# A transformer block on one core: the last matrix product by row tiles, the residual added by transfers, the row factors asked for last

## The chip, the cores and the metric

The kernel runs on one core of a Trainium2 chip. That core has a matrix engine (PE, TensorE), a vector engine (DVE), a scalar engine (ACT), a general engine (POOL, GpSimd) and a queue engine (SP) that mostly issues DMA transfers; ACT and POOL can issue transfers too, on queues of their own. Each engine runs its instructions strictly in the order in which they were put into its program, so an instruction that waits holds everything behind it on that engine. The metric is the device time of one execution in microseconds (us).

## What is computed

The block is one layer of a flow-matching backbone on 512 tokens of width 2048: a modulated norm, a combined input projection for gated linear attention and a gated short convolution, an output projection with a gated residual, then a second modulated norm, a SwiGLU feed-forward with hidden width 5632 and another gated residual, and a final norm. The change lies in the last three of these, cut to what matters:

```python
x_next = x + gt1 * mix                                   # 512 x 2048
h2 = modulate(rmsnorm(x_next, norm2_g), sh2, sc2)
x_next = x_next + gt2 * ((silu(h2 @ wg) * (h2 @ wu)) @ wd)   # wd: 5632 x 2048
out = rmsnorm(x_next, final_g)    # x * rsqrt(mean(x*x, row) + 1e-6) * final_g
```

`gt2` and `final_g` are vectors over the 2048 columns; the norm's factor is one number for each of the 512 rows.

## The kernel before, in words

**Products in pieces.** Operands are float32 and are split into a high and a low part in a reduced format (`split`: ACT casts the high part, L102, DVE subtracts to get the low part, L103), and three matmuls replace one (`mm3`). The order within `mm3` is low part of the stationary operand by high part of the weights, high by low, high by high; the first matmul of a product thus needs only the cast of the weights, the second needs DVE's low part as well.

**Seven products for eight.** The product with `wd` runs in 2 by 2 blocks by `seven`, which needs seven block products with sums and differences of blocks. The hidden width is cut into three groups (`GROUPS`: `nu` = 4, 4 and 3 units of 2 x 256), and for each group `g` the output columns are cut into two halves `p` of 1024. For each `(g, p)`, `seven` goes through steps "1", "5", "63", "7", "24", or in the last one (`g` = 2, `p` = 1, called `fast`) "1", "5", "63", "2", "7", "4". In each step and for each unit `u` it asks for a weight tile (512 KB: `held` into `ch` in steps 1 and 5, `load_raw` into `raw` in steps 63 and 24, four buffers), forms differences of weight tiles on DVE, splits, and runs 12 matmuls of 512 columns. Stationary operands A11, S1, S2, S4, S3, A12, A22 (tiles `a0` to `a6`, a high and a low part each) were written to memory earlier (`opd`) and are brought back by `load_ops`, 256 KB each, by SP.

**What sets the order.** SP's program follows the order in which the kernel's code asks for loads. The `before` table of `seven` names places, a step or a step and a unit, at which something is asked for ahead of that step. On the other engines the tile framework's scheduler places the instructions by its own estimates of time; the written order is only its input.

**The end of a column block.** `upd` adds a finished accumulator to the output tiles `y[row tile][column block]` (128 x 512 each, 4 row tiles by 4 blocks). When the last addition to a tile is done, `finish_block` loads the block's saved residual `xnd` into a tile of pool `big` (SP, L1110), multiplies `y` by `gt2` (DVE, L1111), adds the residual (DVE, L1112), and squares and sums it (ACT, L1113). When the second half of the columns has the blocks of a pair of row tiles, `finish_rows` works out the row factors (`row_scale`: a reduction, a chain of 128 x 2 operations on DVE and a square root on ACT) and multiplies eight tiles by row factor and `final_g` at once (DVE, L1120), each followed by its output transfer from POOL (L1121).

## Time and profile before

| what | value |
| --- | --- |
| time, median of 3 runs | 2346.79 us (2343.20 to 2351.29) |
| the profiled execution | 2344.56 us, its span 2342.8 us |
| granted TensorE clock, mean | 0.986 |
| PE busy | 2257.2 us, 96% of the span |
| DVE / ACT / POOL busy | 1667.6 / 1012.4 / 139.3 us |
| DMA | 431.43 MB, mean 184 GB/s |

The span runs from the first to the last instruction in the trace. A row of a timeline has the start, the duration, the engine, the line, the operation with output and inputs, how many instructions stand in the row, and in brackets how long the engine was idle ahead of it and which instruction ended that. `SPq` is SP's queue of transfers to issue. A row of a table of windows has the busy time and count of each engine in a stretch of the span, then the clock granted to PE (PEclk), the busy share of the 16 DMA engines and what they moved.

### The profile page before, as it was taken

The page shows a single profiled execution, that of the slowest core. Times are in us where ns is not written, and L with a number is a line of the kernel's source. Part 1 is how long each engine was busy: PE and PEld are TensorE (multiplying, and loading weights), DVE is VectorE, ACT ScalarE, POOL GpSimd, SP SyncE. Part 2 cuts the span into 40 slices and gives each one's busy share as a digit, 9 for nine tenths or more (in the row PEclk, how much of TensorE's full clock was granted, in tenths as well). Part 3 has the DMA queues.
Part 4 walks back from the last instruction along what each step waited for, and adds up shares of the span by engine and source line. Part 5 has one row for each costly group of instructions (what it writes and reads, how often), then busy time and mean ns, then how long its engine had stood idle before and what let it go on. Part 6 is the DMA issues. An engine that isn't in the chain of part 4 may idle for free.

```text
span 2342.8 us, 27643 instructions
## 1 busy us (share of the span) xinstructions
PE 2257.2 (96%) x10232; PEld 1794.3 (77%) x10232; DVE 1667.6 (71%) x2046; ACT 1012.4 (43%) x1365; POOL 139.3 (6%) x186
## 2 busy tenths in 40 slices
PE   8999999999989999989999999999999999999996
PEld 4766667787877778767888888888888878888875
DVE  3566164655655757769888788878887867787898
ACT  3432155233232334485554555455545544443343
POOL 2433000000000000000000000000000000000001
PEclk9999999999999999989999999999999999999998
DMA  9774465665656654533434643464346585755634
GB/s 329 229 245 135 144 225 162 206 194 190 221 187 204 191 179 172 188 107 128 160 123 147 207 144 123 147 206 144 122 148 207 187 316 173 279 181 192 253 128 143
DMA packets 161620, 431.43 MB, mean 184 GB/s; under 512 B 17868, under 2 KB 38636, under 8 KB 161357
## 3 DMA queue, kind: packets, MB, share of 16 engines
q1 hardware_dynamic: 141612, 380.87, 49.1%
q0 software_dynamic: 8720, 28.58, 3.2%
q10 hardware_dynamic: 11152, 20.21, 2.3%
q8 instruction: 81, 1.33, 0.2%
q14 instruction: 55, 0.44, 0.1%
HBM read 380.82 MB, written 48.78 MB: 183 GB/s over the span
## 4 chain that ended last, share of the span: by engine, by line
issue 42%; PE 10%; DVE 2%; POOL 2%; ACT 1%; DMA 0%; POOLq 0%; ACTq 0%; DVEq 0%
PE acc L90 10%; POOL opd L1002 1%; DVE wlo L103 1%; POOL out L1121 0%; PE pt L988 0%; DVE ch L812 0%; ACT big L906 0%; ACT whi L102 0%; DMA raw<-wu 0%; DVE a4l L103 0%; DVE s L739 0%; DVE a6l L103 0%; DVE ch L793 0%; DVE a3l L103 0%; DVE ch L798 0%
## 5 line engine op out<-in xcount | busy, mean ns | idle before, releaser
L102 ACT CAST whi<-ch 128x1024 fp32r<-128x1024 f32 x350 | 368.8, 1055 | 425.9 <-PE acc L90 348.5
L103 DVE TENSOR_TENSOR wlo<-ch,whi 128x1024 fp32r<-128x1024 f32 x350 | 426.1, 1222 | 139.0 <-ACT whi L102 137.9
L102 ACT CAST whi<-raw 128x1024 fp32r<-128x1024 f32 x252 | 264.1, 1052 | 414.9 <-PE acc L90 244.9
L103 DVE TENSOR_TENSOR wlo<-raw,whi 128x1024 fp32r<-128x1024 f32 x252 | 308.9, 1227 | 186.6 <-ACT whi L102 186.1
L374 DVE CUSTOM_DVE_ANT_0 raw<-raw,cbc 128x1024 f32<-128x1024 f32 x128 | 156.4, 1224 | 190.1 <-DMA raw<-wm 187.6
L90 PE MATMUL acc<-hhl,whi 128*128 128x512 f32 x640 | 201.6, 396 | 0.0
L90 PE MATMUL acc<-hhi,wlo 128*128 128x512 f32 x320 | 135.8, 426 | 14.0 <-DVE wlo L103 13.0
L90 PEld LDWEIGHTS acc<-hhl,whi 128*128 128x128 f32 x640 | 122.3, 191 | 28.2 <-issue 2.5
L90 PE MATMUL acc<-whi,a6l 128*128 128x512 f32 x312 | 122.5, 394 | 8.5 <-ACT whi L102 7.5
L90 PE MATMUL acc<-hhl,wlo 128*128 128x512 f32 x320 | 128.3, 401 | 0.0
L90 PE MATMUL acc<-hlo,whi 128*128 128x512 f32 x320 | 127.7, 399 | 0.2 <-DVE hlo L108 0.2
L90 PE MATMUL acc<-hhi,whi 128*128 128x512 f32 x320 | 127.4, 398 | 0.0
L90 PE MATMUL acc<-wlo,a6h 128*128 128x512 f32 x312 | 123.0, 394 | 2.2 <-DVE wlo L103 2.1
L90 PE MATMUL acc<-wlo,a0h 128*128 128x512 f32 x312 | 122.6, 393 | 2.1 <-DVE wlo L103 2.1
L90 PE MATMUL acc<-whi,a6h 128*128 128x512 f32 x312 | 122.3, 392 | 0.0
L90 PE MATMUL acc<-whi,a5l 128*128 128x512 f32 x312 | 121.9, 391 | 0.0
L90 PE MATMUL acc<-wlo,a5h 128*128 128x512 f32 x312 | 121.7, 390 | 0.0
L90 PE MATMUL acc<-whi,a5h 128*128 128x512 f32 x312 | 121.6, 390 | 0.0
L90 PE MATMUL acc<-whi,a0h 128*128 128x512 f32 x312 | 121.5, 389 | 0.0
L90 PE MATMUL acc<-whi,a0l 128*128 128x512 f32 x312 | 121.3, 389 | 0.0
L90 PE MATMUL acc<-whi,a2l 128*128 128x512 f32 x280 | 109.1, 392 | 4.8 <-ACT whi L102 4.8
L90 PE MATMUL acc<-wlo,a2h 128*128 128x512 f32 x280 | 110.2, 394 | 1.4 <-DVE wlo L103 1.4
(305 smaller groups left out, 4747.6 us busy)
## 6 DMA issues: line engine op xcount, KB each, us to landing
raw<-wm SPq DMA_DIRECT2D x128, 512.0 KB, 4.7
raw<-wu SPq DMA_DIRECT2D x92, 512.0 KB, 3.8
ch<-wu SPq DMA_DIRECT2D x88, 512.0 KB, 4.0
raw<-wc SPq DMA_DIRECT2D x48, 512.0 KB, 4.0
raw<-wd SPq DMA_DIRECT2D x47, 512.0 KB, 6.0
ch<-wd SPq DMA_DIRECT2D x44, 512.0 KB, 5.9
opd<-oh ACTq DMA_DIRECT2D x77, 256.0 KB, 3.0
opd<-ol POOLq DMA_DIRECT2D x77, 256.0 KB, 3.3
```

What stands on the lines that cost most here:

```text
L90: nc.tensor.matmul(o, l, r, start=start, stop=stop, skip_group_check=True)
L102: nc.scalar.copy(hi, src)
L103: (eng or nc.vector).tensor_tensor(lo, src, hi, op=ALU.subtract)
L374: nc.vector.tensor_tensor_reduce(out=w, in0=w, in1=cbc[:, hf * 1024 : hf * 1024 + 1024], scale=1.0, scalar=0.0, op0=ALU.mult, op1=ALU.add, ...
L1002: nc.gpsimd.dma_start(opd[j][i, 1].rearrange("p k t -> p (k t)"), lo.bitcast(F32))
```

## The change

There are four edits, all in the product with `wd`.

1. In the first half of each group's columns (`p` = 0), the loads of S3 (`a4`) are asked for in step "63" ahead of its last unit, and those of A12 and A22 (`a5`, `a6`) ahead of step "7". Before, S3 came ahead of step "5", and A12 and A22 ahead of step "63".
2. `finish_block` no longer loads the residual into a tile of its own and no longer adds it on DVE. `residual` multiplies `y` by `gt2` on DVE, and a transfer issued by POOL adds `xnd` into `y` (`accum_op`). The square on ACT and a new multiplication by `final_g` on DVE follow it.
3. `finish_rows` applies the row factors on ACT, eight plain scalings, instead of with `final_g` on DVE.
4. In the last projection the last step is "4r": the splits of its three weight tiles come first, then all products of row tile 0, then all of row tile 1, and after each of the two `finish_tile` does the rest of that row tile: scale, add, square, `final_g`, a row factor of its own, and four scalings shared by ACT and DVE, with the output transfers on SP, POOL and ACT. The residuals of these two tiles are put in earlier, ahead of step "7".

```diff
@@ seven
-        def product(i, u, r, acc, first):
+        def parts(r):
             hi = wpool.tile([P, 1024], F32R, tag="whi", name="whi", bufs=3)
             lo = wpool.tile([P, 1024], F32R, tag="wlo", name="wlo", bufs=3)
             split(hi, lo, r)
+            return hi, lo
+
+        def product(i, u, r, acc, first, rows=(0, 1)):
+            hi, lo = r if type(r) is tuple else parts(r)
             if first and u == 0:
                 acc += [bank8("acc"), bank8("acc")]
-            for t in range(2):
+            for t in rows:
...
                     if "4" in step:
                         tt(a[u], c, a[u], op=ALU.subtract)
+                    if step == "4r":
+
+                        b[u] = parts(a[u])
+                        for t in range(2) if end else ():
+                            for v in range(nu):
+                                product(A22, v, b[v], X, False, (t,))
+                            after["c21"](t, X[t])
+                    elif "4" in step:
                         product(A22, u, a[u], X, False)
@@ the product with wd
             def before_63():
...
-                if p == 0:
-                    load_ops(g, A12, A22)
-                else:
+                if p:
                     load_ops(g + 1, A11)

             def before_5():
-                if p == 0:
-                    load_ops(g, S2, S4, S3) if g == 0 else load_ops(g, S3)
                 if p == 0 and g == 0:
+                    load_ops(g, S2, S4)
                     back(NPU - 1)

             before = {"5": before_5, "63": before_63}
+            if p == 0:
+                before["63", nu - 1] = lambda: load_ops(g, S3)
+                before["7", 0] = lambda: load_ops(g, A12, A22)
...
-                    if fast and c == 0 and not new:
-                        finish_rows(tt0)
                 return f
+
+            def residual(tt, d):
+
+                o = y[tt][d]
+                nc.vector.tensor_tensor(o, o, gt2b[d], op=ALU.mult)
+                nc.gpsimd.dma_start(o, xnd[tt, :, d * NB : d * NB + NB], accum_op=ALU.add)

             def finish_block(tt, d):
                 o = y[tt][d]
-                x = big()
-                nc.sync.dma_start(x, xnd[tt, :, d * NB : d * NB + NB])
-                nc.vector.tensor_tensor(o, o, gt2b[d], op=ALU.mult)
-                nc.vector.tensor_tensor(o, o, x, op=ALU.add)
-                nc.scalar.activation(x, o, AF.Square, accum_out=ssf[:, tt, d : d + 1])
+                residual(tt, d)
+                nc.scalar.activation(big(), o, AF.Square, accum_out=ssf[:, tt, d : d + 1])
+                nc.vector.tensor_tensor(o, o, fgb[d], op=ALU.mult)

             def finish_rows(tt0):
                 r = row_scale(ssf, tt0, 2)
                 for t in range(2):
                     for d in range(NBD):
                         o = y[tt0 + t][d]
-                        nc.vector.scalar_tensor_tensor(o, o, r[:, t : t + 1], fgb[d], op0=ALU.mult, op1=ALU.mult)
+                        nc.scalar.activation(o, o, AF.Copy, scale=r[:, t : t + 1])
                         nc.gpsimd.dma_start(out[tt0 + t, :, d * NB : d * NB + NB], o)
+
+            def finish_tile(t, acc):
+
+                if t == 0:
+                    finish_rows(0)
+                tt, d = 2 + t, 2 * p
+                o, g = y[tt][d], row2k("g21")
+                nc.vector.tensor_tensor(g, acc, gt2b[d], op=ALU.mult)
+                nc.vector.tensor_tensor(o, o, g, op=ALU.add)
+                nc.scalar.activation(acc, o, AF.Square, accum_out=ssf[:, tt, d : d + 1])
+                nc.vector.tensor_tensor(g, o, fgb[d], op=ALU.mult)
+                r = row_scale(ssf, tt, 1)
+                for n, (dd, o) in enumerate(((0, y[tt][0]), (3, y[tt][3]), (1, y[tt][1]), (2, g))):
+                    if n % 2:
+                        nc.vector.tensor_scalar(o, o, r[:, 0:1], None, op0=ALU.mult)
+                    else:
+                        nc.scalar.activation(o, o, AF.Copy, scale=r[:, 0:1])
+                    (nc.sync, nc.gpsimd, nc.scalar, nc.sync)[n].dma_start(out[tt, :, dd * NB : dd * NB + NB], o)
+
+            if fast:
+                before["7"] = lambda: [residual(2 + t, 2 * p) for t in range(2)]

             seven(A, lambda b, u: wd[w0 + b * nu + u], nk, {
...
-                "u3": upd(2, 1, False), "c11": upd(0, 0, False), "c21": upd(2, 0, g == 0)},
-                ("1", "5", "63", "2", "7", "4") if fast else ALL_STEPS, before)
+                "u3": upd(2, 1, False), "c11": upd(0, 0, False), "c21": finish_tile if fast else upd(2, 0, g == 0)},
+                ("1", "5", "63", "2", "7", "4r") if fast else ALL_STEPS, before)
```

**DVE, first group, step 1.** These rows are DVE's in the stretch from the first weight tile's low part of `g` = 0, `p` = 0 to the second one's (`wlo_14133`); `L832`/`L845` and `L1036`/`L1049` are the end of the gate and up products. Before:

```order
L103 TENSOR_TENSOR wlo_14113<-ch_14110,whi_14112 128x1024 [waits DMAHW4_49,Activation_49]
L832 TENSOR_TENSOR u1_13535<-u1_13535,acc_13913 128x512 [waits DMASW3_49,PE_49]
L832 TENSOR_TENSOR u1_13536<-u1_13536,acc_13914 128x512 [waits PE_49]
L103 TENSOR_TENSOR wlo_14133<-ch_14130,whi_14132 128x1024 [waits DMAHW5_49,Activation_49]
L1036 TENSOR_TENSOR u1_13535<-u1_13535,u2_13791 128x512 [waits Activation_49]
```

Now:

```order
L103 TENSOR_TENSOR wlo_14113<-ch_14110,whi_14112 128x1024 [waits DMAHW4_49,Activation_49]
L845 TENSOR_TENSOR u1_13535<-u1_13535,acc_13913 128x512 [waits DMASW3_49,PE_49]
L845 TENSOR_TENSOR u1_13536<-u1_13536,acc_13914 128x512 [waits PE_49]
L792 TENSOR_TENSOR ch_14110<-ch_14238,ch_14110 128x1024 [waits DMAHW0_49,DVE_49]
L1049 TENSOR_TENSOR u1_13535<-u1_13535,u2_13791 128x512 [waits Activation_49]
L1049 TENSOR_TENSOR u1_13536<-u1_13536,u2_13792 128x512 [waits Activation_49]
L1049 TENSOR_TENSOR g21_14055<-g21_14055,v_13637 128x512 [waits DMASW1_49,Activation_49]
L1049 TENSOR_TENSOR g21_14058<-g21_14058,v_13638 128x512 [waits DMAHW5_49,Activation_49]
L103 TENSOR_TENSOR wlo_14133<-ch_14130,whi_14132 128x1024 [waits DMAHW5_49]
```

A difference of step 5 (L792), which waits for the transfer of its weight tile, and the four products of L1049 now stand ahead of the second low part of step 1.

**ACT, last group, from step 7 to step 24 of the first half.** `whi_16809` is the last cast of step 7, `whi_16839` the first of step 24. `y_14062` and `y_14066` are the block that step 63 finishes, `y_14070` and `y_14074` the one that step 7 finishes. Before:

```order
L102 CAST whi_16809<-ch_16610 128x1024 [waits DVE_49,PE_49]
L1113 ACTIVATE big_16766,ssf_14077<-y_14062 128x512 [waits DMAHW6_49,DVE_49]
L1113 ACTIVATE big_16772,ssf_14077<-y_14066 128x512 [waits DMAHW7_49,DVE_49]
L102 CAST whi_16839<-raw_16837 128x1024 [waits DMAHW2_49,PE_49,Activation_49]
L102 CAST whi_16858<-ch_16500 128x1024 [waits PE_49,Activation_49]
L102 CAST whi_16876<-raw_16874 128x1024 [waits DMAHW3_49,DVE_49,PE_49]
L1113 ACTIVATE big_16826,ssf_14077<-y_14070 128x512 [waits DMAHW0_49,DVE_49]
L1113 ACTIVATE big_16832,ssf_14077<-y_14074 128x512 [waits DMAHW1_49,DVE_49]
```

Now:

```order
L102 CAST whi_16809<-ch_16598 128x1024 [waits DVE_49,PE_49]
L1127 ACTIVATE big_16744,ssf_14077<-y_14062 128x512 [waits DMASW7_49]
L1127 ACTIVATE big_16750,ssf_14077<-y_14066 128x512 [waits DMASW0_49]
L1127 ACTIVATE big_16828,ssf_14077<-y_14070 128x512 [waits DMASW1_49]
L1127 ACTIVATE big_16834,ssf_14077<-y_14074 128x512 [waits DMASW2_49]
L102 CAST whi_16839<-raw_16837 128x1024 [waits DMAHW6_49,DVE_49,PE_49]
L102 CAST whi_16858<-ch_16500 128x1024 [waits DVE_49,PE_49,Activation_49]
```

The squares of the block that step 7 finishes stood behind the third cast of step 24 and stand ahead of the first now; each waits for a transfer of POOL's queue (`DMASW`).

**ACT, the end.** `rs_m_17415` and `rs_m_17458` belong to the row factors of row tiles 2 and 3, `rs_r_17384` holds those of row tiles 0 and 1. Now (before, ACT ended with the squares of `y_14071` and `y_14075` and one square root):

```order
L143 ACTIVATE rs_t_17416<-rs_m_17415 128x1 [waits DVE_49]
L1146 ACTIVATE acc_16975,ssf_14077<-y_14075 128x512 [waits DVE_49]
L1135 ACTIVATE y_14061<-y_14061,rs_r_17384 128x512 [waits DVE_49]
...
L1135 ACTIVATE y_14068<-y_14068,rs_r_17384 128x512
L1153 ACTIVATE y_14069<-y_14069,rs_r_17417 128x512 [waits DVE_49]
L1153 ACTIVATE y_14070<-y_14070,rs_r_17417 128x512
L143 ACTIVATE rs_t_17459<-rs_m_17458 128x1
L1154 DMA out<-y_14070 128x512 [waits Activation_49]
L1153 ACTIVATE y_14073<-y_14073,rs_r_17460 128x512 [waits DVE_49]
```

The square root that the last row tile's factor needs stands behind eight scalings of row tiles 0 and 1 and two of row tile 2.

## The prediction

> **What bounds the kernel now.** I read the page's busy times first, then a table of windows over the product with `wd`, then the timelines of the engines where PE has gaps.
>
> ```profile
> PE 2257.2 (96%) x10232; PEld 1794.3 (77%) x10232; DVE 1667.6 (71%) x2046; ACT 1012.4 (43%) x1365; POOL 139.3 (6%) x186
> 1885.00:1900.00 15.00, 15.00 (x68) 12.43 (x67) 11.45 (x13) 7.76 (x10) 0.00 (x0) 1.00 1.04 392
> 1917.00:1921.00 4.00, 2.73 (x7) 1.87 (x8) 4.00 (x6) 2.90 (x5) 0.63 (x2) 0.62 0.54 201
> 1921.00:1925.00 4.00, 4.00 (x11) 3.15 (x10) 3.94 (x5) 2.23 (x3) 0.54 (x1) 0.52 0.67 222
> 1925.00:1940.00 15.00, 15.00 (x67) 12.39 (x66) 13.17 (x13) 5.86 (x6) 0.00 (x0) 1.00 0.33 101
> 2245.00:2253.00 8.00, 8.00 (x37) 6.63 (x36) 7.04 (x10) 4.39 (x7) 0.00 (x0) 1.00 1.02 407
> 2260.00:2280.00 20.00, 16.40 (x71) 12.88 (x70) 19.74 (x24) 8.27 (x15) 0.00 (x0) 1.00 0.00 1
> ```
>
> PE is busy for 96% of the span and issues about 4.5 matmuls per us wherever it runs freely (67 in 15 us, a pitch of 0.227 us). The change leaves the number of matmuls alone, so it can only act on PE's gaps and on what follows PE's last matmul. The product with `wd` begins at 1890.6 us. Three places matter: the stop near 1917, DVE's full stretch from 2260 to 2280, and the end.
>
> The stop near 1917, by timelines of PE, SP and DVE:
>
> ```profile
> 1913.92 0.39 PE L90 MATMUL acc<-whi,a1h 128*128 128x512 f32 x1
> 1917.45 0.79 PE L90 MATMUL acc<-whi,a2l 128*128 128x512 f32 x2 [3.15 <-ACT whi L102]
> 1919.06 0.80 PE L90 MATMUL acc<-wlo,a2h 128*128 128x512 f32 x1 [0.82 <-DVE wlo L103]
> 1924.77 0.42 PE L90 MATMUL acc<-whi,a3h 128*128 128x512 f32 x1
> 1885.33 0.32 SPq L1060 DMA_DIRECT2D a4h<-opd  x1
> 1890.75 2.51 SPq L758 DMA_DIRECT2D ch<-wd  x4
> 1906.79 3.04 SPq L118 DMA_DIRECT2D raw<-wd  x4
> 1912.79 1.22 DVE L793 TENSOR_TENSOR ch<-raw,ch 128x1024 f32<-128x1024 f32 x1 [4.25 <-DMA raw<-wd]
> ```
>
> SP issues `a4` at 1885.33 and only at 1906.79, behind `a5` and `a6`, the first weight tile of step 63. DVE waits 4.25 us for it, ACT and PE in turn. The matmul at 1924.77 is the sixteenth after the one at 1913.92; 16 pitches would put it at 1917.55, so the stop costs 7.2 us. Of this 3.15 and 0.82 are idle. The other 3.2 is a slow clock: 0.62 and 0.52 are granted in the two windows up to 1925, and 1.00 after. In 2260 to 2280, gaps of 2.14 and 1.46 us (quoted below) leave the clock at 1.00.
>
> The Trainium skill explains this in "TensorE: Matmul & The Clock Gate" (section "What's actually happening"): the clock halves after an idle window of about 3.4 us and comes back after a busy one, the windows running free. The 3.15 us gap followed by half speed agrees.
>
> **Edit 1, loads behind weights: gain 7.2, give back 2.5.** Now SP issues the four `ch` loads of step 5 at the place of `a4`, from 1885.33, and three `raw` loads behind them. Seven issues at the 0.7 us that the row of four shows (2.51 us and the last one's return) end at about 1891, 16 us ahead of 1906.79, and DVE began to wait for the first `raw` at 1908.5 (1912.79 − 4.25). The fourth stands behind eight `a4` that may wait for free tiles, but it belongs to the step's last unit, three units of 5.4 us later. The stop goes: −7.2. What is late next is DVE in step 1.
>
> ```profile
> 1889.19 1.22 DVE L103 TENSOR_TENSOR wlo<-ch,whi 128x1024 fp32r<-128x1024 f32 x1 [0.30 <-ACT whi L102]
> 1890.33 1.28 DVE L1036 TENSOR_TENSOR u<-u,u 128x512 f32<-128x512 f32 x2
> 1890.62 0.39 PE L90 MATMUL acc<-whi,a0l 128*128 128x512 f32 x1
> ch<-wd SPq DMA_DIRECT2D x44, 512.0 KB, 5.9
> ch<-wu SPq DMA_DIRECT2D x88, 512.0 KB, 4.0
> ```
>
> Ahead of the second low part of step 1 now stand a difference that waits for the new `ch` and four products of 0.60. The tile is issued at 1885.33 and lands by the row's median of 5.9 at 1891.2 (with 4.0, at 1889.3). Then 1.14 for the difference, 2.4 for the four products and 1.2 for the low part make 1896.0. PE wants it one product (12 × 0.227 = 2.7) and one matmul after 1890.62, at 1893.6. So 2.4 us of new idle, 0.5 with the short landing; I take 2.5. If it trips the clock it costs 3.2 more, but 2.14 did not. Groups 1 and 2 show no PE gap at this place, and their loads stay far ahead: nothing. Net −4.7, between −6.7 and −1.5.
>
> **Edit 2, the residual by transfers: +12.** It removes 16 SP loads and 16 additions of 0.69 from DVE, and adds 16 POOL transfers and 16 multiplications by `final_g`, so DVE's work hardly changes. But the square on ACT now waits for a transfer that can start only when the block is done. At the boundary from step 7 to 24 in the last group ACT holds both squares ahead of the cast that PE needs next. Rows of before at that place:
>
> ```profile
> 2244.93 1.28 DVE L1100 TENSOR_TENSOR y<-y,acc 128x512 f32<-128x512 f32 x2
> 2246.12 1.29 DVE L1111 TENSOR_TENSOR y<-y,hbig 128x512 f32<-128x512 f32 x2
> 2245.16 0.39 PE L90 MATMUL acc<-whi,a5l 128*128 128x512 f32 x1
> 2245.36 1.06 ACT L102 CAST whi<-raw 128x1024 fp32r<-128x1024 f32 x1 [1.61 <-PE acc L90]
> 2248.05 0.64 ACT L1113 ACTIVATE big<-y 128x512 f32<-128x512 f32 x1 [1.63 <-DVE y L1112]
> L1121 POOL DMA_DIRECT2D out<-y x16: 542/542/551, 2322.1 to 2338.2; - x16
> DMA to landing us min/median/max: 2.6/3.1/3.4
> DMA to landing us min/median/max: 2.6/4.0/8.9
> ```
>
> (The last two rows are the landings of `out` from POOL and of all transfers of `xnd`.) PE went from step 7 to step 24 at 2245.16 with no gap. Now additions and multiplications of both tiles end at 2247.4, POOL issues, the transfer lands, the square takes 0.64 and the cast 1.05. No transfer of the trace adds into its target. The nearest are POOL's plain writes, 2.6 to 3.4 us, and the transfers of the same `xnd`, 2.6 to 8.9; it reads two operands, and the window from 2245 moves 407 GB/s, so I take 4.0. The cast ends at 2247.4 + 4.0 + 0.64 + 1.05 = 2253.1, a gap of 7.9 us where there was none. The low part comes a further 0.8 after (as in the row at 1919.06), and the clock costs what it cost at 1917, 3.2. Sum 11.9. By the bounds: landing 2.6 and half of the clock's loss, 6.5 + 0.8 + 1.6 = 8.9; landing 8.9 gives 12.8 + 0.8 + 3.2 = 16.8. Nothing covers this: PE has no other product in its order. A gain is excluded, since PE never waited here.
>
> The other blocks of the last half:
>
> ```profile
> 2266.95 0.50 PE L90 MATMUL acc<-wlo,a0h 128*128 128x512 f32 x1 [2.14 <-DVE wlo L103]
> 2274.18 0.50 PE L90 MATMUL acc<-wlo,a1h 128*128 128x512 f32 x1 [1.46 <-DVE wlo L103]
> 2315.56 0.47 PE L90 MATMUL acc<-whi,a6l 128*128 128x512 f32 x1 [0.71 <-DVE y L1100]
> 2319.89 0.50 PE L90 MATMUL acc<-wlo,a6h 128*128 128x512 f32 x1 [0.87 <-DVE wlo L103]
> ```
>
> These four gaps, 5.2 us, come from DVE's queue of additions and splits. The additions of the residual leave it; squares that wait for landings enter ACT's queue between casts, with a cast between two of them and a step between two blocks. I take +1: gaps of the same sum, and one wait longer by the 0.9 by which 4.0 exceeds 3.1. Bounds are −2 (the first gap goes) and +6 (four squares, each 1.5 later).
>
> **Edits 3 and 4, the end: +0.5.** Rows of before:
>
> ```profile
> 2324.80 0.39 PE L90 MATMUL acc<-whi,a6h 128*128 128x512 f32 x1
> 2332.38 5.39 DVE L1120 SCALAR_TENSOR_TENSOR y<-y,rs_r,hbig 128x512 f32<-128x512 f32 x8
> 2333.53 5.18 POOL L1121 DMA_DIRECT2D out<-y  x8 [6.09 <-DVE y L1120]
> L906 ACT ACTIVATE hbig<-xn,rs_r x4: 707/708/720, 992.8 to 994.6; 128x512 f32<-128x512 f32 x4
> 2331.78 0.16 DVE L146 TENSOR_TENSOR rs_t<-rs_t,rs_m 128x2 f32<-128x2 f32 x1
> 2325.00:2330.00 5.00, 0.19 (x1) 0.00 (x0) 4.95 (x9) 0.62 (x2) 1.94 (x4) 0.76 0.84 311
> ```
>
> PE ends at 2325.2 and the span 17.6 us later: 7.2 up to the eight multiplications at 2332.38, 5.4 for them, and 5 from there to the end. Now row tile 1's path after PE's end is: three DVE operations of 0.69 (a multiplication, the addition, the one by `final_g`) and four small ones until the factors of row tiles 0 and 1 are there, 2.7. Then ACT runs eight scalings and two more at a pitch of 0.60 (the row of L906: four starts within 1.8 us) before the square root: 6.0. Then 0.2 + five small operations of 0.2 + two scalings of 0.6 make 2.4, and issue, landing and end another 5: 16.1. But all 16 output tiles, 4.2 MB, now leave after PE's end instead of half of them; at 311 GB/s that is 13.5 us from the first scaling's transfer, 4 us after PE's end, and with 1.5 to close the span 19. I take 18.1, between the two and nearer to the transfers, which cannot be avoided: +0.5, between −1.5 and +2.5. Step "4r" makes row tile 0 ready 11 matmuls ahead of PE's end instead of 6 (1.1 us), which buys nothing, as ACT's order makes the last factor wait.
>
> The Trainium skill, in "DMA: Bandwidth & Descriptors" (section "Issuing engines are not separate DMA queues"), says that transfers from SP, ACT and POOL run on the same 16 engines; it speaks against a gain from spreading them, and by it the end would be the 19.
>
> **The sum.** −7.2 + 2.5 + 11.9 + 1 + 0.5 = +8.7 on the profiled 2344.56 us, which lies 2.2 below the median of 2346.79. From the median: **2355.5 us**. Its own range, with all lower and all upper bounds added: −1.3 to +23.8, 2345.5 to 2370.6.
>
> **Rivals.**
> *Faster: PE hardly stops at the boundary, and the gain of edit 1 stands* (0.15). It needs a landing below every one of POOL's rows and no slow clock: with half of 2.6 the gap is 5.2 and a low part soon behind it, +5.5. With edit 1 at −6.7, the other blocks at −2 and an end that follows ACT's chain alone with its eight scalings run before PE ends (−1.5 and up to −2.7 more), that is −7.4: 2339. For it: DVE's queue is full in 2260 to 2280, and taking additions out of it may shift more than I count. Against it: ACT's order has both squares ahead of the cast, and no landing in the trace is that short.
> *Gains and losses cancel* (0.33): landing 2.6 with half of the clock's loss, +8.9 − 6.7 + 0 + 0 = +2, 2349. For it: POOL's own rows centre on 3.1. Against: the transfer reads its target too.
> *The accumulating transfer is slow, 7 us or more* (0.15): the boundary costs 10.9 + 4.0 = 14.9, the other blocks +6, the end +2; with −4.7 that is +18, 2365. For: `xnd` rows reach 8.9 under load.
> *The loads don't move what they should*: held SP waits would leave the `raw` loads as late as before, so that the stop stays and step 1 has no new gap: 8.7 + 4.7 = +13.4, 2360 (0.05). Against: SP's program has three `raw` loads ahead of all `a4`.
>
> **How the numbers follow.** A change of 0.3%, 7 us, is about what can be told from none. Slower by more, above 2353.8: 0.52, of which the forecast has 0.32 and the last two rivals 0.2. Within: 0.33, the cancelling case. Faster: 0.15. The range runs from 2342, which leaves out most of the faster case, to 2368, a little under the sum of all upper bounds.
>
> **What would show it.** Right: in the first group no gap of PE in step 63 and a gap of 2 to 3 us in the first two units of step 1; in the last group, between the last matmul of step 7 and the first of step 24, a gap of 6 to 9 us ended by ACT's cast, a granted clock near 0.5 behind it, and ACT waiting for POOL's transfer of `xnd`; a landing of those transfers near 4; 18 us from PE's last matmul to the end. Wrong: no PE gap at that boundary, or landings under 2.6, or the end shorter by more than 3 us.

## The result, and the profile after

The changed kernel takes 2368.11 us (median of 5 runs, 2364.86 to 2368.68) against 2349.84 us for the kernel before (5 runs beside them): a ratio of 1.0081 with a 95% interval of 1.0068 to 1.0094, about 19 us more. The forecast was 2355.5 us, so it had the direction and less than half of the size; the measured time lies 0.1 us above its range.

In the two profiled executions the program up to the product with `wd` is the same instruction by instruction, yet that product begins at 1894.90 us instead of 1890.62. These 4.3 us have no part in the change. From the first matmul of that product to the end of the span it is 471.4 us now (2366.3 − 1894.90) and 452.2 before: +19.2, in agreement with the times.

The same stretches as in the prediction, in a table of windows of the kernel after (columns as there):

```profile
1885.00:1900.00 15.00, 13.23 (x59) 10.63 (x57) 9.42 (x11) 7.55 (x10) 0.00 (x0) 1.00 1.04 398
1917.00:1925.00 8.00, 8.00 (x37) 6.64 (x36) 7.47 (x9) 5.34 (x8) 0.54 (x1) 1.00 0.65 226
2240.00:2260.00 20.00, 6.42 (x25) 4.46 (x24) 7.17 (x11) 4.19 (x10) 2.36 (x3) 0.75 0.42 79
2260.00:2280.00 20.00, 19.27 (x79) 15.85 (x80) 14.87 (x17) 7.95 (x8) 1.76 (x2) 0.91 0.41 136
```

The stop near 1917 is gone: PE is busy for all of 1917 to 1925, at a clock of 1.00. Instead PE stands idle for two thirds of 2240 to 2260, and the clock is reduced there. PE's timeline after has these rows with gaps, between its first and last matmul of the product:

```profile
1894.90 0.39 PE L90 MATMUL acc<-whi,a0l 128*128 128x512 f32 x1
...
1900.28 0.50 PE L90 MATMUL acc<-wlo,a0h 128*128 128x512 f32 x1 [2.04 <-DVE wlo L103]
...
2258.65 1.22 PE L90 MATMUL acc<-whi,a5l 128*128 128x512 f32 x2 [13.45 <-ACT whi L102]
2260.73 0.80 PE L90 MATMUL acc<-whi,a6l 128*128 128x512 f32 x1 [0.86 <-ACT whi L102]
...
2287.03 0.50 PE L90 MATMUL acc<-wlo,a0h 128*128 128x512 f32 x1 [3.05 <-DVE wlo L103]
2293.31 0.50 PE L90 MATMUL acc<-wlo,a1h 128*128 128x512 f32 x1 [1.45 <-DVE wlo L103]
2297.87 0.50 PE L90 MATMUL acc<-whi,a2l 128*128 128x512 f32 x1 [1.53 <-ACT whi L102]
...
2346.50 0.39 PE L90 MATMUL acc<-whi,a6h 128*128 128x512 f32 x1
```

Both kernels run 1848 matmuls in this product, so the start of the n-th can be compared. Differences by stretch, after less before:

| stretch | before, us | after, us | difference |
| --- | --- | --- | --- |
| matmuls 1 to 600 (the old stop, the new gap of 2.04) | 145.1 | 140.7 | −4.4 |
| 601 to 1500 | 204.0 | 204.0 | 0.0 |
| 1501 to 1560 (end of step 7, first half of step 24, last group) | 13.6 | 30.4 | +16.8 |
| 1561 to the last (rest of step 24, then the last half of the columns) | 71.5 | 76.6 | +5.1 |
| last matmul to the end of the span | 18.0 | 19.8 | +1.8 |

One boundary makes most of the loss. It is where the prediction put the new stop, but 13.45 us long instead of 7.9. These are DVE's, ACT's and POOL's timelines of the kernel after at that place; L1113 is the last addition to `y`, L1121 the multiplication by `gt2`, L1122 the accumulating transfer, L1127 the square and L1128 the multiplication by `final_g` behind it:

```profile
2244.38 0.63 ACT L1127 ACTIVATE big<-y 128x512 f32<-128x512 f32 x1 [6.25 <-DMA y<-xnd]
2245.14 0.69 DVE L1128 TENSOR_TENSOR y<-y,hbig 128x512 f32<-128x512 f32 x1 [4.93 <-ACT big L1127]
2247.12 0.63 ACT L1127 ACTIVATE big<-y 128x512 f32<-128x512 f32 x1 [2.01 <-DMA y<-xnd]
2247.87 0.69 DVE L1128 TENSOR_TENSOR y<-y,hbig 128x512 f32<-128x512 f32 x1 [2.04 <-ACT big L1127]
2248.48 0.68 DVE L1113 TENSOR_TENSOR y<-y,acc 128x512 f32<-128x512 f32 x1
2250.52 0.69 DVE L1121 TENSOR_TENSOR y<-y,hbig 128x512 f32<-128x512 f32 x1
2250.29 0.87 POOL L1122 DMA_DIRECT2D y<-xnd  x1 [9.64 <-DVE y L1121]
2251.62 0.85 POOL L1122 DMA_DIRECT2D y<-xnd  x1 [0.46 <-DVE y L1121]
2254.53 0.63 ACT L1127 ACTIVATE big<-y 128x512 f32<-128x512 f32 x1 [6.69 <-DMA y<-xnd]
2256.94 0.63 ACT L1127 ACTIVATE big<-y 128x512 f32<-128x512 f32 x1 [1.69 <-DMA y<-xnd]
2257.57 1.03 ACT L102 CAST whi<-raw 128x1024 fp32r<-128x1024 f32 x1
```

PE stopped at 2258.65 − 13.45 = 2245.2. The first four rows belong to the block that step 63 finished: its transfers land at 2244.4 and 2247.1, its squares follow, and DVE waits for each of them in L1128. Only then, at 2248.48, does DVE add the block that step 7 finished, 3.3 us after PE stopped with both accumulators complete. Additions and multiplications take until 2251.2 (2.7), the second transfer lands at 2256.94 (5.7 more), and square and cast make 1.7: 13.4.

### The profile page after: what moved, and what is told of

Read it like the earlier page. It is cut to its first block, busy times and chain, and to the rows that moved or that the text cites. A ratio compares the mean times of both kernels' runs of the same rounds, so it can differ in the third digit from the quotient of the medians.

```text
span 2366.3 us, 27658 instructions
## 1 busy us (share of the span) xinstructions
PE 2259.5 (95%) x10232; PEld 1794.5 (76%) x10232; DVE 1661.2 (70%) x2043; ACT 1020.1 (43%) x1378; POOL 149.8 (6%) x196
## 4 chain that ended last, share of the span: by engine, by line
PE 49%; issue 3%; DVE 3%; DMA 1%; ACT 1%; POOL 0%; POOLq 0%; DVEq 0%; ACTq 0%; SPq 0%
PE acc L90 48%; DMA y<-xnd 1%; PE pt L1001 1%; DVE wlo L103 1%; ACT whi L102 0%; DMA ch<-wd 0%; DVE ch L817 0%; DMA a3h<-opd 0%; DVE y L1121 0%; DVE y L1113 0%; ACT big L919 0%; POOL out L1136 0%; DVE y L1128 0%; POOL y L1122 0%; DVE a4l L103 0%
## 5 line engine op out<-in xcount | busy, mean ns | idle before, releaser
L90 PE MATMUL acc<-whi,a5l 128*128 128x512 f32 x312 | 122.5, 394 | 13.4 <-ACT whi L102 13.4
L90 PE MATMUL acc<-wlo,a4h 128*128 128x512 f32 x280 | 109.5, 391 | 2.6 <-DVE wlo L103 2.5
```

The source lines that it names most:

```text
L90: nc.tensor.matmul(o, l, r, start=start, stop=stop, skip_group_check=True)
```

## The experiments

Three theories were on trial. A: the accumulating transfer's landing makes the stop. B: the place of the squares in ACT's order, ahead of the cast, makes it. C, formed on the way: the multiplication by `final_g` behind the square makes it, since DVE waits for ACT there and everything behind it waits too. Times are differences of medians to the kernel before, run on the same chip, with the ratio's interval.

### The residual loaded again

```diff
             def residual(tt, d):
                 o = y[tt][d]
+                x = big()
+                nc.sync.dma_start(x, xnd[tt, :, d * NB : d * NB + NB])
                 nc.vector.tensor_tensor(o, o, gt2b[d], op=ALU.mult)
-                nc.gpsimd.dma_start(o, xnd[tt, :, d * NB : d * NB + NB], accum_op=ALU.add)
+                nc.vector.tensor_tensor(o, o, x, op=ALU.add)
```

> The change with its residual put back: SP loads it into a tile of its own and DVE adds it; the loads behind weights, the multiplication by final_g behind the square and the new end stay. Theory A (the wait for the accumulating transfer makes the stop): ACT still has both squares ahead of the cast at the boundary from step 7 to 24, but they wait only for DVE; its three operations per tile end near 3.4 us after PE stops, square and cast add 1.7: a gap of about 5 instead of 13.45, some 8 us lost with the slow clock, loads -5, end +2: about +5 us on the kernel before. Rival B (the order on ACT and DVE makes the stop whatever brings the residual): the gap stays over 10 and the sum near +18.

Measured: +25.8 us, ratio 1.0119 (1.0102 to 1.0136). Without a single accumulating transfer it is slower than the change. Two of its four stops in PE's timeline, then DVE and ACT ahead of the first of them:

```profile
2280.54 0.80 PE L90 MATMUL acc<-whi,a0l 128*128 128x512 f32 x1 [8.18 <-ACT whi L102]
2350.91 1.22 PE L90 MATMUL acc<-whi,a6l 128*128 128x512 f32 x2 [9.95 <-ACT whi L102]
2277.44 0.69 DVE L1130 TENSOR_TENSOR y<-y,hbig 128x512 f32<-128x512 f32 x1 [0.79 <-ACT big L1129]
2278.05 0.69 DVE L1124 TENSOR_TENSOR y<-y,big 128x512 f32<-128x512 f32 x1
2278.83 0.63 ACT L1129 ACTIVATE big<-y 128x512 f32<-128x512 f32 x1 [1.42 <-DVE y L1124]
2279.46 2.92 ACT L102 CAST whi<-ch 128x1024 fp32r<-128x1024 f32 x3
```

The boundary gap fell to 5.94 us, near the 5 that theory A expected, but new stops came elsewhere. DVE and ACT take turns here: DVE's multiplication (L1130) waits for ACT's square, the next addition (L1124) stands behind that multiplication, the next square waits for that addition, and the casts stand behind all squares. Theory A as the whole cause falls.

### The loads alone

The four lines of edit 1 in the kernel before.

> The kernel before with edit 1 alone, the loads behind weights. Both theories: the stop in step 63 (7.2 us) goes and a gap of about 2.2 comes in step 1, no gap at the boundary from step 7 to 24: -5 us. If the moved loads harm groups 1 and 2, the sum is 0 or more and there are PE gaps near 1960 to 2260.

Measured: −3.9 us, ratio 0.9987 (0.9976 to 0.9997). The gap of step 1 came as forecast (2.25 us lost between two matmuls), the stop of step 63 did not, and nothing happened in groups 1 and 2. Of the 5.0 expected, 2.3 went to reduced clock after gaps: the first 600 matmuls took 142.4 us, 2.7 less than before.

### The accumulating transfer alone

```diff
-                x = big()
-                nc.sync.dma_start(x, xnd[tt, :, d * NB : d * NB + NB])
                 nc.vector.tensor_tensor(o, o, gt2b[d], op=ALU.mult)
-                nc.vector.tensor_tensor(o, o, x, op=ALU.add)
-                nc.scalar.activation(x, o, AF.Square, ...)
+                nc.gpsimd.dma_start(o, xnd[tt, :, d * NB : d * NB + NB], accum_op=ALU.add)
+                nc.scalar.activation(big(), o, AF.Square, ...)
```

> The kernel before with the residual added by accumulating transfers, and nothing else: the loads, the end and the multiplication by final_g with the row factor at the end are those of before. In the order that results the squares of the block that step 7 finishes stand behind three casts of step 24. Theory A (the transfer's landing makes the stop): squares that wait 5 us or more still hold casts somewhere; +8 to +14 us. Rival B (the place of the squares ahead of the cast makes it): no gap over 3 us at that boundary, the sum between 0 and +4.

Measured: +11.1 us, ratio 1.0056 (1.0040 to 1.0071). The sum lies in theory A's range, but no gap at the boundary is over 3 us, as theory B had it. PE loses 2.8 us behind the first product of step 24 and, three casts later, 3.5, each with about 1.7 us of reduced clock behind it. The end takes 22.0 us instead of 18.0, because the last two blocks now wait for a transfer behind their last addition. The change had avoided that last cost by asking for the residuals of those two tiles ahead of step 7.

### Plain transfers in place of accumulating ones

The argument `accum_op=ALU.add` is left out of the change. The transfer then writes `xnd` over `y`, so this kernel leaves out the sum of product and residual; it measures time alone.

> The change with plain transfers in place of the accumulating ones: xnd is written over y, so the sum of product and residual is left out; everything else and its order is as in the change. Theory A1 (an accumulating transfer is slower than a plain one): landings near 3.1 as for the output tiles instead of 4.2, two in a row 0.6 to 1 us apart instead of 2.4; the boundary gap falls from 13.45 to about 8, the sum to +9 to +11. Rival A2 (POOL's queue and the issue cost the time): landings and gap as in the change, +18.

Measured: +13.4 us, ratio 1.0066 (1.0046 to 1.0087). PE's boundary gap, POOL's two issues, and all landings of `xnd`; behind them the landings of the change:

```profile
2255.59 1.22 PE L90 MATMUL acc<-whi,a5l 128*128 128x512 f32 x2 [9.61 <-ACT whi L102]
2248.92 0.55 POOL L1122 DMA_DIRECT2D y<-xnd  x1 [7.88 <-DVE y L1121]
2250.24 0.55 POOL L1122 DMA_DIRECT2D y<-xnd  x1 [0.78 <-DVE y L1121]
DMA to landing us min/median/max: 2.6/3.4/6.6
```

```profile
DMA to landing us min/median/max: 2.6/4.2/7.4
```

An accumulating transfer costs POOL 0.87 us instead of 0.55 and lands 0.8 us later in the median. By the medians that is worth 4.9 us of the 18.3 (18.3 − 13.4), but the intervals of the two ratios overlap, so the size is uncertain; in the traces the boundary stretch is 3.1 us shorter (27.3 against 30.4). The expectation of +9 to +11 was too hopeful, since a plain transfer that is waited for leaves 13.4.

### Another scratch tile for the square

```diff
-                nc.scalar.activation(big(), o, AF.Square, accum_out=ssf[:, tt, d : d + 1])
+                nc.scalar.activation(row2k("sqj"), o, AF.Square, accum_out=ssf[:, tt, d : d + 1])
```

> The change with one edit: the throw-away output of the square in finish_block is taken from the pool of 17 row tiles instead of the pool of 24 that also holds the stationary operands. Its transfers are those of the change, but ACT's order now has the squares of the block of step 7 behind the third and the fourth cast of step 24. Theory B (the place of the squares makes the stop): the boundary gap falls from 13.45 to under 3, the sum from +18 to +2 to +6. Theory A (the slow landing alone makes it): PE still stops for over 8 us near 2245 to 2265, the sum stays over +12.

Measured: +10.3 us, ratio 1.0044 (1.0029 to 1.0060). The order alone was worth 8 us. At the boundary 2.6 and 0.9 us are lost instead of 13.6 and 1.3, and three casts later another 1.3 and 1.0. But +10 remained, more than theory B's +2 to +6, and the longest gap is now at step 1 of the last half. DVE there, and PE:

```profile
2272.61 0.69 DVE L1128 TENSOR_TENSOR y<-y,hbig 128x512 f32<-128x512 f32 x1 [2.05 <-ACT sqj L1127]
2275.67 0.69 DVE L1128 TENSOR_TENSOR y<-y,hbig 128x512 f32<-128x512 f32 x1 [1.77 <-ACT sqj L1127]
2276.28 1.22 DVE L103 TENSOR_TENSOR wlo<-ch,whi 128x1024 fp32r<-128x1024 f32 x1
2277.55 0.80 PE L90 MATMUL acc<-wlo,a0h 128*128 128x512 f32 x1 [4.06 <-DVE wlo L103]
```

DVE waits in L1128 for squares, and the low part for which PE waits stands behind. That made theory C.

### The loads and the accumulating transfer together, with the old end

The edits of the second and third experiment together.

> The kernel before with the loads behind weights and the accumulating transfers, but with the end of before (no final_g behind the square, no scalings on ACT, no row tiles). Either part alone left ACT's order good; together the order puts the squares of the block of step 7 ahead of the first cast of step 24, as in the change. Theory B: the stop at the boundary is back, 9 to 13 us, and the sum is +12 to +18, of which the end edits have no share. If the multiplication by final_g behind the square is needed for the stop, the gap is under 7 and the sum under +9.

Measured: +8.5 us, ratio 1.0038 (1.0026 to 1.0051). Squares ahead of the cast, but no L1128: 8.6 us are lost at the boundary against 13.6 in the change. The gap of 8.44 us lies between the two branches of the expectation (9 to 13, and under 7), so both the place and the multiplication count. The sum is under the +9 of the second branch, and more than half of it is the old end, which takes 22.6 us here instead of 18.0, as in the run with the accumulating transfer alone.

### The residual loaded into one tile

The square's output goes over the loaded tile, as in the kernel before; nothing else differs from the run of +25.8.

> The change with its residual loaded by SP and added on DVE, and the square's output written over the loaded tile as in the kernel before; it differs from the run of +25.8 us only in that the square has no tile of its own. ACT's order has the squares behind the casts again. Theory B: no gap over 3 us at the boundary, loads -4, new end about +1: -5 to +2 in all. If residual loads with final_g behind the square are slow in themselves, the sum stays over +15.

Measured: +0.5 us, ratio 1.0000 (0.9989 to 1.0012). The one tile moved the squares behind casts and was worth 25 us. Why the scheduler places the squares by the choice of a scratch tile, the traces don't show.

This run also bounds theory C. The multiplication by `final_g` stands behind every square here too, but no square waits for a transfer, and PE loses nothing at the boundary (13.6 us for matmuls 1501 to 1560, as before the change). So the multiplication alone makes no stop there; it needs a square that waits for a landing, or one that stands ahead of the cast as in the run of +25.8. The last half of the columns still takes 7.5 us longer than in the kernel before, which the loads and a shorter end (14.4 us) nearly make up.

### Without the multiplication behind the square

`final_g` goes back to the end (DVE, with the row factor). With the other scratch tile:

```diff
                 nc.scalar.activation(row2k("sqj"), o, AF.Square, accum_out=ssf[:, tt, d : d + 1])
-                nc.vector.tensor_tensor(o, o, fgb[d], op=ALU.mult)
...
-                        nc.scalar.activation(o, o, AF.Copy, scale=r[:, t : t + 1])
+                        nc.vector.scalar_tensor_tensor(o, o, r[:, t : t + 1], fgb[d], op0=ALU.mult, op1=ALU.mult)
```

> The change with the square's throw-away tile from the other pool and without the multiplication by final_g behind the square: final_g comes back with the row factor on DVE at the end. Against the run with the other scratch tile alone (+10 us) it takes away only the DVE instructions that wait for ACT's square and so for the landing. Theory C (these hold DVE and with it the low parts of the next half's step 1): the loss there (gaps of 4.2, 1.6 and 1.7 us) falls under that of the kernel before (2.3 and 1.6), the sum to +2 to +5. Rival (ACT's squares that wait for landings hold the casts): the gaps and the +10 stay.

Measured: +1.7 us, ratio 1.0004 (0.9993 to 1.0014). Against the run with L1128, 10.3, nearly everything is gone. The edit also takes the final scalings from ACT back to DVE, which shortens the end from 17.9 to 15.8 us, so 2.1 of the 8.6 us are not the work of L1128. And with the change's own scratch tile, so with the squares still ahead of the cast:

> The change with its own scratch tile, so with the squares of step 7's block still ahead of the first cast of step 24, but without the multiplication by final_g behind the square (it is done with the row factor on DVE at the end). Theory C: at the boundary DVE adds at once and is not held by the square of the block before; the gap falls from 13.45 by the 3.3 us that DVE was late, to 8.5 to 10.5, and the loss in step 1 of the last half from 6 to 3; sum +7 to +11. If the stop is only the place of the squares, the gap stays near 13.45 and the sum near +18.

Measured: +3.6 us, ratio 1.0016 (1.0005 to 1.0027). PE's gap, and DVE's two additions of the same block:

```profile
2249.36 1.22 PE L90 MATMUL acc<-whi,a5l 128*128 128x512 f32 x2 [8.31 <-ACT whi L102]
2239.73 0.69 DVE L1113 TENSOR_TENSOR y<-y,acc 128x512 f32<-128x512 f32 x1 [3.67 <-PE acc L90]
2241.09 0.69 DVE L1113 TENSOR_TENSOR y<-y,acc 128x512 f32<-128x512 f32 x1
```

DVE now waits for PE's accumulators and adds at once, the second time as PE stops (2249.36 − 8.31 = 2241.05); in the change that addition came 4.6 us after the stop. The gap of 8.31 us is a little under the expected 8.5 to 10.5, and the sum under the expected +7 to +11. Together with the change and the run before it the two causes are separated (ratio to the kernel before, less 1, in per mille):

| | squares ahead of the cast | squares behind casts |
| --- | --- | --- |
| with L1128 behind the square | 8.1 | 4.4 |
| without | 1.6 | 0.4 |

L1128 is worth 4.0 to 6.5 per mille (9 to 15 us, of which the moved scalings at the end are 2.1 and 2.4), the place 1.2 to 3.7 (3 to 9 us). The 1.2 is not clear of the noise, since the two intervals overlap. That each costs more where the other is there rests on a difference of 2.5 per mille, about as large as its uncertainty.

### Towards a faster kernel

Half of edit 1, A12 and A22 behind the weights of step 63, S3 where it was:

> The kernel before with half of edit 1: A12 and A22 are asked for behind the weights of step 63, S3 stays ahead of step 5. DVE's order in step 1 is that of before. Expected: no stop in step 63 and no new gap in step 1, -7.2 us, 2 us better than edit 1 whole. If the weights of step 63 still come late behind S3, part of the 7.2 stays.

Measured: −3.8 us, ratio 0.9983 (0.9969 to 0.9997). That is half of the 7.2 expected, and not better than edit 1 whole. In the profiled execution the first 600 matmuls take 139.2 us, 5.9 less than before, and the last half of the columns 1.6 more. Neither the old stop nor the gap in step 1 is there, in windows of this kernel:

```profile
1885.00:1900.00 15.00, 15.00 (x76) 12.69 (x75) 13.58 (x14) 6.47 (x8) 0.00 (x0) 1.00 1.03 402
1900.00:1915.00 15.00, 15.00 (x67) 12.41 (x67) 15.00 (x15) 8.86 (x11) 1.08 (x2) 1.00 0.85 308
1915.00:1930.00 15.00, 15.00 (x68) 12.42 (x67) 11.66 (x13) 8.03 (x11) 0.54 (x1) 1.00 0.54 182
```

With it, three ends by row tiles and no accumulating transfer were tried:

> The kernel before with A12 and A22 asked for behind the weights of step 63 and with a new end: products of the last step by row tiles, each with its own factor, the residual of the last two tiles loaded by SP and added ahead of step 7, final_g still with the row factor on DVE. No accumulating transfer, no final_g behind the square. Stop in step 63 gone: -5 to -7; the end 13 us instead of 18; DVE's eight multiplications of row tiles 0 and 1 stand ahead of two low parts of the last step and may cost PE 0 to 4. Sum -6 to -11 us. If the end is bound by the 16 output transfers, the sum is that of the loads alone, -4.

> As the run with the row tiles, with final_g applied ahead of the factor to column blocks 0 and 1 (eight multiplications on DVE in step 2 of the last half, none behind a square) so that ACT does half of the scalings; four of DVE's stand ahead of two low parts of the last step instead of eight. Sum 2 to 3 us better than with all on DVE: -8 to -13. If DVE is full in step 2, the eight multiplications cost PE there as much as they save at the end.

> As the run with split scalings, but the row factors of row tiles 0 and 1 are asked for last as in the change: no scaling stands ahead of the last low parts, all 16 output transfers leave after PE's end. If transfers bind the end, it takes 13.5 us at 311 GB/s and 15 to 16 in all, against 11 to 13 with half of them sent earlier; PE has no gap in the last step. Sum -5 to -9, 1 to 3 us worse than with the factors asked for early.

Measured: +1.4 us (ratio 1.0010, 0.9999 to 1.0021), −3.9 (0.9990, 0.9978 to 1.0003) and −1.9 (0.9986, 0.9974 to 0.9998). The ends are 14.2, 12.1 and 16.0 us instead of 18.0, but the first pays for it ahead of PE's last product:

```profile
2314.28 5.38 DVE L1155 SCALAR_TENSOR_TENSOR y<-y,rs_r,hbig 128x512 f32<-128x512 f32 x8
2322.05 0.80 PE L90 MATMUL acc<-wlo,a6h 128*128 128x512 f32 x1 [6.59 <-DVE wlo L103]
```

Eight scalings that nothing on PE needs stand ahead of a low part that PE does need. Asking for the row factors late, as the change does, avoids that: the gap there is 1.15 us in the third. All three also have a gap of 2.4 to 2.5 us in step 7 of the last half that the kernel before doesn't have. All three sums miss what was expected of them by 3 us or more. The first is slower than the loads alone (the intervals don't meet); the other two cannot be told from them.

The last kernel has the half of edit 1 and the old end, with `final_g` for column blocks 0 and 1 on POOL behind the square:

```diff
                 nc.scalar.activation(x, o, AF.Square, accum_out=ssf[:, tt, d : d + 1])
+                if d < 2:
+                    nc.gpsimd.tensor_tensor(o, o, fgb[d], op=ALU.mult)
...
-                        nc.vector.scalar_tensor_tensor(o, o, r[:, t : t + 1], fgb[d], op0=ALU.mult, op1=ALU.mult)
+                        if d < 2:
+                            nc.scalar.activation(o, o, AF.Copy, scale=r[:, t : t + 1])
+                        else:
+                            nc.vector.scalar_tensor_tensor(o, o, r[:, t : t + 1], fgb[d], op0=ALU.mult, op1=ALU.mult)
```

> The kernel before with A12 and A22 asked for behind the weights of step 63, and final_g applied to column blocks 0 and 1 by POOL, which is idle there, behind the square; ACT then does half of the final scalings and DVE four instead of eight per pair of row tiles. No wait is added on DVE or ahead of a cast. Loads -4 to -6; the end 14 to 15.5 us instead of 18. Sum -6 to -9 us. If POOL's multiplications (1.4 us each) slow DVE, gaps grow at the start of the last half and the sum is that of the loads alone, -4.

Measured: −3.7 us by medians, ratio 0.9971 (0.9960 to 0.9983), which is −6.8 us; the two estimates differ by 3.1 us, and the interval is 5.4 wide. Only the second lies in the expected −6 to −9, and the end of 16.1 us is longer than the expected 14 to 15.5. It beats both kernels, though its lead on the loads alone lies within the intervals.

## Why the prediction was wrong

**Edit 1** held. The stop of 7.2 us went, and 2.04 us came in step 1 where 2.4 had been worked out, by the chain that was named. Net −4.4 in the traces against −4.7.

**Edit 2's stop** was named at the right place, with the right engine at its end, and it was mis-sized: 16.8 us against 11.9. The step that failed is the sentence that the 16 multiplications by `final_g` leave DVE's work hardly changed. It counted their durations and not their wait. Each stands behind a square that waits for a landing, and DVE's next addition, 3.3 us late, stood behind two of them. That was in DVE's order, and the prediction named nothing that was queued behind them. The gap exceeds the 7.9 us that were worked out by 5.5: 3.3 for DVE's late start, 0.5 for additions and multiplications that take longer, and 1.7 for the landing. Without L1128 (the run of +3.6) the gap is 8.31, so the rest of the chain was nearly right. The landing was the second error: 4.0 was taken and 4.2 is the median, but the second of two in a row is the one that counts, 5.3 us after its issue (2251.62 to 2256.94), 5.7 after its data was ready. The clock cost 1.5 us instead of 3.2 (the eight intervals between matmuls from 2260.73 on, less their pitches), which took some of it back. The rival of a slow transfer at 7 us gave 2365, near the measured time, but by luck: the landings were 4.2 in the median, and the wait that was missing was DVE's.

**The last half** was put at +1 and measured +5.1. The bound of +6 named late squares; what came was L1128 again, and about 2 us of reduced clock behind longer gaps. These are ACT and DVE of the change at the start of the last half:

```profile
2281.85 0.63 ACT L1127 ACTIVATE big<-y 128x512 f32<-128x512 f32 x1 [2.44 <-DMA y<-xnd]
2282.61 0.69 DVE L1128 TENSOR_TENSOR y<-y,hbig 128x512 f32<-128x512 f32 x1 [2.05 <-ACT big L1127]
2284.39 0.63 ACT L1127 ACTIVATE big<-y 128x512 f32<-128x512 f32 x1 [1.82 <-DMA y<-xnd]
2285.15 0.69 DVE L1128 TENSOR_TENSOR y<-y,hbig 128x512 f32<-128x512 f32 x1 [1.25 <-ACT big L1127]
2285.76 1.22 DVE L103 TENSOR_TENSOR wlo<-ch,whi 128x1024 fp32r<-128x1024 f32 x1
```

The low part at 2285.76 is the one that PE waited 3.05 us for. Without L1128, with the same transfers and the squares still ahead of the cast (the run of +3.6), PE has no gap in step 1 and loses 0.7 us twice in step 5.

**The end** was put at +0.5 and measured +1.8. The chain was as worked out: ten scalings on ACT ahead of the last square root, then the transfers.

```profile
2350.74 5.00 ACT L1135 ACTIVATE y<-y,rs_r 128x512 f32<-128x512 f32 x8
2355.65 1.32 ACT L1153 ACTIVATE y<-y,rs_r 128x512 f32<-128x512 f32 x2
2356.87 0.19 ACT L143 ACTIVATE rs_t<-rs_m 128x1 f32<-128x1 f32 x1
```

The scalings began 4.2 us after PE's last matmul started (2350.74 − 2346.50), which is 3.9 after its end and not 2.7. DVE waited 2.01 us for a square in L1128 just ahead of the reduction from which these row factors start (2345.43); what else made the 1.8 was not tested apart.

**Signs.** What the prediction said would show it right is there: the gap in step 1, the stop ended by ACT's cast, ACT waiting for `xnd`, landings near 4. What it called 6 to 9 us was 13.45, and the 18 us at the end were 19.8.

## What to carry to other kernels

When an edit puts a short instruction behind one that waits for a transfer, its price is not its 0.69 us but the wait, paid by everything that stands behind it in that engine's order; ask for each added instruction what it waits for and which instruction that PE needs is next. A transfer in place of an addition pays only if nothing that matters waits for its landing: at the end of this kernel, starting it ahead of the last addition left 17.4 to 19.8 us, and behind it 22.0 and 22.6. Where a scheduler sets the order, the choice of a scratch tile can move an instruction across a cast and be worth as much as the edit itself or more (8 and 25 us here), so the order belongs to what is compared before a price is put on anything.

## What the runs showed of the hardware

An accumulating transfer of 256 KB held POOL for 0.87 us against 0.55 for a plain one, and two issued 1.3 us apart landed 2.4 us apart (2254.53 and 2256.94). In between, these two transfers were all that moved, and they kept the DMA engines busy:

```profile
2252.50:2254.50 2.00, 0.00 (x0) 0.00 (x0) 0.00 (x0) 0.00 (x0) 0.00 (x0) 0.50 0.97 161
```

At a busy share of 0.97 they moved 161 GB/s; the kernel before moved 407 at 1.02 in the window from 2245. So an accumulating transfer held the engines for more than twice as long per byte as that mixed load. In the run with plain transfers, two issued 1.3 us apart landed 1.7 us apart.

The same gap can cost the clock or not. The kernel before has a gap of 2.14 us in step 1 of the last half and keeps a clock of 1.00. The kernel with the loads alone has the same gap, by PE's timeline and a window:

```profile
2268.87 0.50 PE L90 MATMUL acc<-wlo,a0h 128*128 128x512 f32 x1 [2.14 <-DVE wlo L103]
2268.00:2272.00 4.00, 3.13 (x9) 2.46 (x10) 4.00 (x4) 1.25 (x3) 0.00 (x0) 0.69 0.01 2
```

There the matmuls behind it start 0.43 us apart instead of 0.227 for about 3 us, which costs 1.6 us. The Trainium skill, in "TensorE: Matmul & The Clock Gate" (section "What's actually happening"), says that the window in which idleness is judged is about 3.4 us and runs free of the program; that it runs free agrees with the same gap costing nothing in one execution and 1.6 us in another, but a gap of 2.14 us is shorter than the window, and so is, by less, the gap of 3.15 us that the prediction read as agreeing.

POOL's multiplications in the last kernel, at their neighbour DVE's cost:

```profile
2263.09 3.00 POOL L1115 TENSOR_TENSOR y<-y,hbig 128x512 f32<-128x512 f32 x2 [8.41 <-issue]
2263.91 2.72 DVE L1111 TENSOR_TENSOR y<-y,hbig 128x512 f32<-128x512 f32 x2
```

Two multiplications of DVE that take 1.29 us in the kernel before take 2.72 in this execution while POOL works beside them, and a gap in step 1 of the last half grew from 2.14 to 3.56 us.
